# Seven block products in place of eight for the second layer's input projection

## The chip, the cores and the metric

The kernel runs on one core of one Trainium2 chip. The metric is the device time of one execution in microseconds: the median of several runs, lower is better. A profile of one more execution gives the span (from the first to the last instruction) and the trace of every instruction, wait and transfer.

## The reference

A trunk of two residual layers over 512 tokens of 1024 channels, in float32. Each layer computes `x <- x + RMSNorm_post(mixer(RMSNorm_pre(x)))`. The first layer's mixer has two groups of heads (a gated matrix memory and a stick-breaking attention); the change leaves its arithmetic alone. The second layer is what matters here:

```python
def odd_layer(x, pre_g, post_g, w_in, pool_w, pool_scale, w_out):
    h = rmsnorm(x, pre_g)                       # 512 x 1024
    u = h @ w_in                                # 1024 x 4096
    p, z = u[..., :2048], u[..., 2048:]
    pooled = multiscale_pool(p as 4 groups of 512 channels)   # windows 2, 4, 8, 16
    mixed = einsum('bsgc,gce->bsge', pooled, pool_w) * pool_scale
    y = (mixed * silu(z)) @ w_out               # 2048 x 1024
    return x + rmsnorm(y, post_g)
```

`multiscale_pool` subtracts each value from the mean of the last 2, 4, 8 or 16 tokens of its channel.

## The kernel before

Every matrix product is made of three: each float32 operand is kept as two parts in the type float32r, a high part (the value rounded) and a low part (what is left), and `mm3` accumulates high x high, high x low and low x high in PSUM. `split` makes the parts: ACT copies the value into the high tile, which rounds it, and DVE subtracts that from the value into the low tile. For weights, `load` has SP's queue bring a block of 1 MB into one of two `w32` buffers, and `halves` splits a piece of it into one of four pairs of tiles, tagged `wh` and `wl`. A buffer comes free when its last reader is done, and whoever needs it next waits for that.

The code is written for a framework that allocates the tiles, puts in the waits, and orders the instructions of each engine ahead of time with a planner's own model of their costs; each engine then runs its list strictly in that order. `act` adds order among functions that need a table, so that ACT loads each table once for a run of them.

The first layer ends with its output projection (`out_steps`, `out_tile`, L537), in two halves of 256 tokens. `finish_even` then does, for each of four tiles of 128 tokens, the post-norm with the residual (`post`, into `xn`) and the second layer's pre-norm (`prenorm`): square, root, scaling, transposes by TensorE into a PSUM bank with the tag `sc`, and a split into `hTh` and `hTl`, which hold the normed input with channels on the partitions, as eight blocks of 128 channels by 512 tokens.

The second layer runs over four groups, one for each window. A group has four column tiles (128 channels each) of p and four of z. `col_load` loads two column tiles and makes their halves; `col_proj` (L189 to L191, matmuls at L95 to L97) does 8 x 3 matmuls of 128x512 for one tile into one of two `pj` banks. For p, ACT copies the bank into a `win` tile with 16 zeros ahead (L674), and DVE makes the window sums by doubling shifts (L684), mends the first tokens (L689, L690), and subtracts (L691); the result is split into `pph` and `ppl` (tags `phi` and `plo`, six buffers each). For z, `project2` yields the banks and ACT applies Silu into `sz` tiles (six buffers). Then the group's mixing matrix is loaded and split into two pairs, and four products of 4 x 3 matmuls each (`mx`, in `ac` banks) follow, which DVE scales and gates into `y32` (L713). In the first group, whose input is only half there when it begins, p goes over the tokens in two halves of 256 columns. Last come the output projection of the second layer, `finish_odd`, and the stores.

GpSimd (POOL) does masks, memsets and, in the first layer, the running sum of the weights of the matrix memory (L381); its queue issues no transfers. `y32` holds the first layer's output and, later, the second's, as 16 tiles of channels by 512 tokens.

Of the kernel before, what the change touches and what calls it, by code (L numbers as in the profile page):

```python
# [5 lines left out]
F32 = mybir.dt.float32  # L6
# [30 lines left out]
def body(nc, tc, x, pre_g, post_g, w_in, conv, b_i, b_f, hn_g, w_out, w_in_c, pool_w,  # L37
# [6 lines left out]
    with base as base, psum as psum, dram as dram:  # L44
# [10 lines left out]
        # functions that need a table run in the order they are written, so that each  # L55
        # table is loaded once for a run of them
# [21 lines left out]
        def load(parts, a, n, name):  # L78
            """Weights as they come, rows of n columns for each of a row tiles."""
# [25 lines left out]
        # the first layer's input and gate rows stand where its output goes later  # L105
# [8 lines left out]
        # constants  # L114
# [21 lines left out]
        # per-channel vectors, one transpose  # L136
# [24 lines left out]
        def prenorm(xt, xs, tt, gain, name, parts=1):  # L161
# [10 lines left out]
            for half in range(2):  # L172
# [26 lines left out]
        with tc.tile_pool(name="att", bufs=1) as at:  # L199
# [11 lines left out]
            # first pre-norm, and the values of four heads as its tokens come  # L211
# [206 lines left out]
            class Stick:  # L418
                """One head of stick-breaking attention, key blocks from the last to the first."""
# [120 lines left out]
            def y_split(half, c, tiles, name):  # L540
                """Two channel tiles of y, for one half of the tokens."""
# [82 lines left out]
        with tc.tile_pool(name="odd", bufs=1) as od:  # L624
            def gains(g, name):
                t = od.tile([P, D], F32, tag="gain", bufs=2, name=name)
# [3 lines left out]
            def xs(name): return od.tile([P, D], F32, tag="xs", bufs=2, name=name)  # L630

            def ytiles(n):
                return (od.tile([P, S], F32R, tag="phi", bufs=6, name=f"yh_{n}"),
                        od.tile([P, S], F32R, tag="plo", bufs=6, name=f"yl_{n}"))
# [5 lines left out]
            def finish_even(ps, tt):  # L640
                xt = od.tile([P, D], F32, tag="xt", bufs=2, name=f"xe{tt}")
                nc.sync.dma_start(xt, xr[:, tt])
                t = xs(f"xse{tt}")
                post(ps, t, gpo, xt, xn[:, tt], f"e{tt}")
                prenorm(xn[:, tt], t, tt, gpr, f"p1{tt}")
# [7 lines left out]
            gpo1 = gains(post_g[1], "g_post1")  # L653
            for g, w in enumerate(WINDOWS):
                pooled = []
                cur4 = []
                for j in range(4):
# [4 lines left out]
                wj = [w for i in range(2)  # L662
                      for w in col_load(w_in_c[0, :, 512 * g + 256 * i:512 * g + 256 * i + 256], f"p{g}{i}")]
                if g == 0:
                    wj = [w() for w in wj]
                    steps = [(j, wj[j], n) for n in range(2) for j in range(4)]
                else:
                    steps = [(j, wj[j], None) for j in range(4)]
                for j, wt, n in steps:
                    wt = wt() if n is None else wt  # L670
                    n0, n1 = (0, S) if n is None else (256 * n, 256 * n + 256)
# [84 lines left out]
```

## Time and profile before

| | |
|---|---|
| median of 3 runs | 919.13 us (918.66 to 919.36) |
| span of the profiled execution | 916.9 us; with the 2.2 us by which the median stands above it, 919.1 us |
| TensorE busy | 904.5 us (99%), 4453 matmuls |
| DVE, ACT, POOL busy | 533.8, 461.5, 51.9 us |
| mean granted TensorE clock | 0.994 |
| moved by DMA | 98.88 MB, 108 GB/s on average |

The profile's own record of the time is the span; what lies around it (start and end of the program) is only in the runs. A line of the groups reads: source line, engine, operation, output <- inputs, shape, count, then busy time in us and mean duration in ns, then how long the engine had been idle just before these instructions and what ended that. In a timeline the columns are start and length in us. In a row for a stretch of time stand its length, then busy time and count for TensorE, its weight loads, DVE, ACT and POOL, then the granted clock, the busy share of the 16 DMA engines, and GB/s. A row on DMA issues ends with the size and the median time from issue to landing.

### The profile page before, as it was taken

The numbers are of one execution on the slowest core, as the hardware profiler recorded it, in microseconds if no ns is written. First come the engines' busy times: TensorE is split into PE (matmuls) and PEld (weight loads), VectorE is DVE, ScalarE is ACT, GpSimd is POOL, SyncE is SP. The second block draws the span as 40 slices with busy tenths as digits, with TensorE's granted clock in tenths as the row PEclk, the third lists the DMA queues.
The fourth block names the chain that finished last, engine by engine and source line by source line (L and its number), as shares of the span: only waits on it lengthen the run. The fifth ranks groups of instructions, "written<-read, shape, count | busy, mean of one in ns | idle before, by whom it ended". The sixth has DMA issues, their size and how long they took to land.

```text
span 916.9 us, 11439 instructions
## 1 busy us (share of the span) xinstructions
PE 904.5 (99%) x4453; PEld 759.6 (83%) x4453; DVE 533.8 (58%) x817; ACT 461.5 (50%) x766; POOL 51.9 (6%) x189
## 2 busy tenths in 40 slices
PE   8999999999999999999999999999999999999996
PEld 6788889889988898898898878898888888888885
DVE  5435556567876675764764828665462745737542
ACT  6426666766668464464565536553231422335331
POOL 2001111101101101001000000000000000000000
PEclk8999999999999999999999999999999999999999
DMA  8231321212122332324221456624223333326331
GB/s 299 84 101 49 91 85 54 88 51 82 59 92 90 129 93 95 98 78 133 92 87 52 158 183 229 204 78 136 92 91 93 92 92 92 98 87 229 114 115 47
DMA packets 67126, 98.88 MB, mean 108 GB/s; under 512 B 2848, under 2 KB 54136, under 8 KB 67072
## 3 DMA queue, kind: packets, MB, share of 16 engines
q1 hardware_dynamic: 65888, 98.08, 32.9%
q8 instruction: 35, 0.57, 0.3%
q10 hardware_dynamic: 1184, 0.08, 0.1%
q14 instruction: 19, 0.16, 0.1%
HBM read 96.02 MB, written 2.13 MB: 107 GB/s over the span
## 4 chain that ended last, share of the span: by engine, by line
PE 97%; DMA 1%; DVE 1%; ACT 0%; issue 0%; DVEq 0%; POOL 0%; POOLq 0%
PE op L537 10%; PE oq L537 10%; PE ps_z L97 3%; PE ps_qa L97 3%; PE ps_qa L95 3%; PE ps_qa L96 3%; PE ps_z L95 3%; PE ps_z L96 3%; PE ps_p_None L96 2%; PE ps_p_None L95 2%; PE ps_p_None L97 2%; PE psv_va L95 2%; PE psv_va L97 2%; PE psv_va L96 2%; PE ps_zb L95 2%; PE mx L97 2%
## 5 line engine op out<-in xcount | busy, mean ns | idle before, releaser
L97 PE MATMUL ps_qa<-hTh,wl_qa 128*128 128x512 f32 x128 | 50.3, 393 | 0.0
L95 PE MATMUL ps_qa<-hTh,wh_qa 128*128 128x512 f32 x128 | 50.2, 393 | 0.0
L97 PE MATMUL ps_z<-hTh,wl_z 128*128 128x512 f32 x128 | 50.2, 393 | 0.0
L96 PE MATMUL ps_qa<-hTl,wh_qa 128*128 128x512 f32 x128 | 50.2, 392 | 0.0
L95 PE MATMUL ps_z<-hTh,wh_z 128*128 128x512 f32 x128 | 50.2, 392 | 0.0
L96 PE MATMUL ps_z<-hTl,wh_z 128*128 128x512 f32 x128 | 50.2, 392 | 0.0
L71 ACT ACTIVATE wh_p<-w_p 128x1024 fp32r<-128x1024 f32 x16 | 17.0, 1059 | 60.9 <-PE mx L96 31.9
L72 DVE TENSOR_TENSOR wl_wo_e<-w_wo_e,wh_wo_e 128x1024 fp32r<-128x1024 f32 x28 | 34.2, 1232 | 21.9 <-ACT wh_wo_e L71 21.9
L71 ACT ACTIVATE wh_wo_e<-w_wo_e 128x1024 fp32r<-128x1024 f32 x28 | 29.3, 1058 | 30.3 <-DMA w_wo_e<-in_w_out_ab 15.6
L72 DVE TENSOR_TENSOR wl_p<-w_p,wh_p 128x1024 fp32r<-128x1024 f32 x16 | 19.6, 1223 | 35.1 <-ACT wh_p L71 35.1
L537 PE MATMUL op<-wl_wo_e,yh_e 128*128 128x512 f32 x120 | 39.0, 396 | 0.0
L537 PE MATMUL op<-wh_wo_e,yl_e 128*128 128x512 f32 x120 | 38.8, 395 | 0.0
L537 PE MATMUL op<-wh_wo_e,yh_e 128*128 128x512 f32 x120 | 37.8, 396 | 0.0
L95 PE MATMUL ps_p_None<-hTh,wh_p 128*128 128x512 f32 x96 | 37.7, 393 | 0.0
L96 PE MATMUL ps_p_None<-hTl,wh_p 128*128 128x512 f32 x96 | 37.7, 393 | 0.0
L97 PE MATMUL ps_p_None<-hTh,wl_p 128*128 128x512 f32 x96 | 37.7, 392 | 0.0
L67 ACT ACT_TABLE_LOAD x28 | 35.9, 1283 | 1.3 <-PEq L742 0.8
L97 PE MATMUL psv_va<-wh_va,hTl 128*128 128x256 f32 x128 | 36.1, 282 | 0.0
L95 PE MATMUL psv_va<-wh_va,hTh 128*128 128x256 f32 x128 | 36.1, 282 | 0.0
L96 PE MATMUL psv_va<-wl_va,hTh 128*128 128x256 f32 x128 | 36.1, 282 | 0.0
L317 DVE SCALAR_TENSOR_TENSOR cv<-u,vecs,cv 128x511 f32<-128x511 f32 (+2 forms) x48 | 35.4, 748 | 0.4
L72 DVE TENSOR_TENSOR wl_wo_o<-w_wo_o,wh_wo_o 128x1024 fp32r<-128x1024 f32 x20 | 24.2, 1223 | 18.9 <-ACT wh_wo_o L71 18.9
(310 smaller groups left out, 2659.7 us busy)
## 6 DMA issues: line engine op xcount, KB each, us to landing
w_wo_e<-in_w_out_ab SPq DMA_DIRECT2D x14, 1024.0 KB, 4.9
w_wo_o<-in_w_out_c SPq DMA_DIRECT2D x12, 1024.0 KB, 4.7
w_qa<-in_w_in_ab SPq DMA_DIRECT2D x8, 1024.0 KB, 5.0
w_p<-in_w_in_c SPq DMA_DIRECT2D x8, 1024.0 KB, 5.4
w_z<-in_w_in_c SPq DMA_DIRECT2D x8, 1024.0 KB, 5.4
w_qb<-in_w_in_ab SPq DMA_DIRECT2D x4, 1024.0 KB
w_kb<-in_w_in_ab SPq DMA_DIRECT2D x4, 1024.0 KB, 5.0
w_zb<-in_w_in_ab SPq DMA_DIRECT2D x4, 1024.0 KB, 4.9
```

Source lines behind the costliest of these rows:

```text
L67: link(A.preload_act_table_set(TABLE[func]))
L71: A.activation(hi, src, AF.Copy)
L72: V.tensor_tensor(lo, src, hi.bitcast(F32), op=ALU.subtract)
L95: T.matmul(dst, lhsT=ah, rhs=bh, start=first, stop=False, **kw)
L96: T.matmul(dst, lhsT=ah, rhs=bl, start=False, stop=False, **kw)
L97: T.matmul(dst, lhsT=al, rhs=bh, start=False, stop=last, **kw)
L317: V.scalar_tensor_tensor(acc[:, j:], u[:, :S - j], cw(3 - j, c), acc[:, j:], op0=ALU.mult, op1=ALU.add)
L537: T.matmul(ps[a][n], lhsT=l[:, ta], rhs=r[:, 0, n * 512:n * 512 + 512], start=(first and l is yh and r is wh), stop=(last and l is yl))
```

## The change

Strassen's scheme in Winograd's form multiplies two 2 x 2 block matrices with seven block products. Here the blocks are: of a weight block of 1024 x 256, two halves of the rows by its two column tiles (a11, a12, a21, a22, 512 x 128 each); of the input, two halves of the channels by two halves of the tokens (512 x 256 each). The new function `strassen2` computes two column tiles for all tokens with seven `product`s of 4 x 3 matmuls of 128x256, in place of two `col_proj` of 8 x 3 matmuls of 128x512. It is called for z in all four groups and for p in groups 1 to 3, 14 calls. The p of the first group keeps its former form.

- The four sums of weight blocks are formed by POOL into `ws` tiles (three buffers). `first` (a11, a21) and `fourth` (a22) are split as before, by ACT and DVE. `second` and `third`, which are the sums, are split by `halves_dma`: ACT writes the negated rounded sum into the low tile and the rounded sum into the high tile, and a transfer that POOL issues adds the sum to the low tile.
- The four sums of input blocks are formed once, by `hidden_sums`, after the first group's p: DVE adds, `split` makes the parts, in eight `big` tiles. They are formed from unrounded values, which `prenorm` now keeps in unused parts of `y32` with one more ACT copy per half tile (`keep`).
- The products accumulate in turn in two halves of banks, `pa` (`pj`) and `pe` (`xb`), with `pb` (`xa`) for the second. What is in `pa` or `pe` between products is copied out by ACT (`t1`, `t2`, `t5`) or read by DVE while the next product runs into another bank.
- Tiles: `gain`, `xs` and `xt` become one tag `big` with eight buffers; `phi` and `plo` go from six to five, `sz` from six to four; POOL's scratch for transfers is set to 2048. The load of `gpo1` stands behind the last group. The two edge operations of the pooling go from DVE to POOL.

```diff
-        def prenorm(xt, xs, tt, gain, name, parts=1):
+        def prenorm(xt, xs, tt, gain, name, parts=1, keep=None):
...
-                split(tp.rearrange("p (a n) -> p a n", a=4), hTh[dst], hTl[dst])
+                tp = tp.rearrange("p (a n) -> p a n", a=4)
+                split(tp, hTh[dst], hTl[dst])
+                if keep is not None:
+                    A.activation(keep[:, half * 4:half * 4 + 4], tp, AF.Copy)
...
+            def big(name, dtype=F32): return od.tile([P, D], dtype, tag="big", bufs=8, name=name)
...
-                prenorm(xn[:, tt], t, tt, gpr, f"p1{tt}")
+                n0 = tt % 2 * P
+                prenorm(xn[:, tt], t, tt, gpr, f"p1{tt}", 1,
+                        y32[:, tt // 2 * 8:tt // 2 * 8 + 8, n0:n0 + P])
...
+            hs = {"11": hblock(0, 0), "21": hblock(1, 0), "22": hblock(1, 1)}
+
+            def ws(name): return od.tile([P, 8, P], F32, tag="ws", bufs=3, name=name)
+
+            def hidden_sums():
+                raw = {}
+                b11, b21, b12, b22 = quarter(0, 0), quarter(1, 0), quarter(0, 1), quarter(1, 1)
+                for n in ("d3", "d1", "n2", "t4"):
+                    raw[n] = ws(f"raw_{n}")...
+                    hs[n] = [big(f"{n}{e}", F32R).rearrange("p (a n) -> p a n", a=4) for e in "hl"]
+                    if n == "d3":
+                        V.tensor_tensor(raw[n], b22, b12, op=ALU.subtract)
+                    elif n == "d1":
+                        V.tensor_tensor(raw[n], b11, b12, op=ALU.subtract)
+                    elif n == "n2":
+                        V.scalar_tensor_tensor(raw[n], raw["d3"], -1.0, b11, op0=ALU.mult, op1=ALU.subtract)
+                    else:
+                        V.scalar_tensor_tensor(raw[n], raw["n2"], -1.0, b21, op0=ALU.mult, op1=ALU.subtract)
+                    split(raw[n], *hs[n])
+
+            def halves_dma(w, name):
+                n = w.shape[1] * w.shape[2]
+                wh, wl = (t[:, :n] for t in whl(name))
+                w = w.rearrange("p a n -> p (a n)")
+                A.activation(wl, w, AF.Copy, scale=-1.0)
+                A.activation(wh, w, AF.Copy)
+                G.dma_start(wl, w, accum_op=ALU.add)
+                return tuple(t.rearrange("p (a n) -> p a n", n=P) for t in (wh, wl))
+
+            def strassen2(src, name, dsts, silu=False):
+                w = load(lambda t: [(nc.sync, t, src)], 8, 256, name)
+                a11, a12, a21, a22 = (w[:, 4 * k:4 * k + 4, m * P:m * P + P]
+                                      for m in range(2) for k in range(2))
+                sums = [ws(f"ws{i}_{name}") for i in range(2)]
+                s1, s2, s3, s4 = sums[0][:, 4:], sums[0][:, :4], sums[1][:, :4], sums[1][:, 4:]
+                G.tensor_tensor(s1, a21, a22, op=ALU.add)
+                G.tensor_tensor(s2, s1, a11, op=ALU.add)
+                G.tensor_tensor(s3, a11, a21, op=ALU.add)
+                G.tensor_tensor(s4, a12, s2, op=ALU.add)
+                first = halves(w[:, :, :P], f"{name}_a")
+                second, third = (halves_dma(t, f"{name}_{n}") for t, n in zip(sums, "bc"))
+                fourth = halves(a22, f"{name}_d")
+
+                def product(ps, wt, k0, b, start, stop):
+                    (wh, wl), (bh, bl) = wt, hs[b]
+                    for k in range(4):
+                        mm3(ps, (wh[:, k0 + k], wl[:, k0 + k]), (bh[:, k], bl[:, k]),
+                            start and k == 0, stop and k == 3, skip_group_check=True)
+
+                def part(i): return od.tile([P, 256], F32, tag="part", bufs=3, name=f"pt{i}_{name}")
+
+                pa, pb, pe = (f(f"ps{n}_{name}")[:, :256] for f, n in ((pj, "a"), (xa, "b"), (xb, "e")))
+                t1, t2, t5 = part(1), part(2), part(5)
+                product(pa, first, 0, "11", True, True)
+                A.activation(t1, pa, AF.Copy)
+                product(pb, first, 4, "21", True, True)
+                V.tensor_tensor(dsts[0][:, :256], pb, t1, op=ALU.add)
+                product(pa, second, 0, "n2", False, True)
+                A.activation(t2, pa, AF.Copy)
+                product(pe, second, 4, "d1", True, True)
+                A.activation(t5, pe, AF.Copy)
+                product(pa, third, 0, "d3", False, True)
+                V.scalar_tensor_tensor(dsts[1][:, 256:], pa, -1.0, t5, op0=ALU.mult, op1=ALU.subtract)
+                product(pe, third, 4, "22", False, True)
+                V.tensor_tensor(dsts[0][:, 256:], pe, t2, op=ALU.add)
+                product(pa, fourth, 0, "t4", False, True)
+                if silu:
+                    act(dsts[0], dsts[0], AF.Silu)
+                    act(dsts[1][:, 256:], dsts[1][:, 256:], AF.Silu)
+                    act(dsts[1][:, :256], pa, AF.Silu, scale=-1.0)
+                else:
+                    A.activation(dsts[1][:, :256], pa, AF.Copy, scale=-1.0)
...
-                    steps = [(j, wj[j], None) for j in range(4)]
-                for j, wt, n in steps:
-                    wt = wt() if n is None else wt
...
+                    hidden_sums()
                 else:
+                    for i in range(2):
+                        strassen2(wsrc[i], f"p{g}{i}", [t[:, 16:] for t in cur4[2 * i:2 * i + 2]])
...
-                    V.tensor_tensor(sm[:, :e], sm[:, :e], invc[:, :e], op=ALU.mult)
-                    V.tensor_tensor(sm[:, :e], sm[:, :e], p32[:, :e], op=ALU.subtract)
+                    G.tensor_tensor(sm[:, :e], sm[:, :e], invc[:, :e], op=ALU.mult)
+                    G.tensor_tensor(sm[:, :e], sm[:, :e], p32[:, :e], op=ALU.subtract)
...
-                for j, ps in enumerate(p for i in range(2) for p in project2(
-                        w_in_c[0, :, 2048 + 512 * g + 256 * i:2304 + 512 * g + 256 * i], f"z{g}{i}")):
...
+                for i in range(2):
+                    pair = [od.tile([P, S], F32, tag="sz", bufs=4, name=f"sz{4 * g + 2 * i + j}")
+                            for j in range(2)]
+                    strassen2(w_in_c[0, :, 2048 + 512 * g + 256 * i:2304 + 512 * g + 256 * i],
+                              f"z{g}{i}", pair, True)
+                    sz.extend(pair)
...
+            gpo1 = gains(post_g[1], "g_post1")
...
-                t, q = xs(f"xo{tt}"), od.tile([P, D], F32, tag="xt", bufs=2, name=f"xq{tt}")
+                t, q = big(f"xo{tt}"), big(f"xq{tt}")
...
+                    dynamic_dma_scratch_size=2048)
```

More of the change, by code (lines that the diff above doesn't have):

```diff
@@ L625, in gains @@
             def gains(g, name):
[L626 removed]
+                t = big(name)
                 nc.sync.dma_start(t, g.partition_broadcast(P))
                 return t
[L630 removed]
+            def big(name, dtype=F32): return od.tile([P, D], dtype, tag="big", bufs=8, name=name)
             def ytiles(n):
[L633 to L634 removed]
+                return (od.tile([P, S], F32R, tag="phi", bufs=5, name=f"yh_{n}"),
+                        od.tile([P, S], F32R, tag="plo", bufs=5, name=f"yl_{n}"))
             ready = y_split(1, EVEN2[0], ytiles("first"), "e")
@@ L651, in body, with quarter, hblock @@
                       lambda a: finish_even(ps1[a], 2 + a))
-            gpo1 = gains(post_g[1], "g_post1")
+            def quarter(k, n): return y32[:, 8 * n + 4 * k:8 * n + 4 * k + 4, 0:256]
+            def hblock(k, n):
+                ix = (slice(None), slice(4 * k, 4 * k + 4), slice(256 * n, 256 * n + 256))
+                return hTh[ix], hTl[ix]
+            hs = {"11": hblock(0, 0), "21": hblock(1, 0), "22": hblock(1, 1)}
+            def ws(name): return od.tile([P, 8, P], F32, tag="ws", bufs=3, name=name)
```

29 lines of the change are left out of this document (12 added, 17 removed).

## The prediction

> **What bounds the kernel now.** I read the page's totals first, then the chain, then TensorE's own waits.
>
> ```profile
> span 916.9 us, 11439 instructions
> PE 904.5 (99%) x4453; PEld 759.6 (83%) x4453; DVE 533.8 (58%) x817; ACT 461.5 (50%) x766; POOL 51.9 (6%) x189
> PEclk8999999999999999999999999999999999999999
> PE 97%; DMA 1%; DVE 1%; ACT 0%; issue 0%; DVEq 0%; POOL 0%; POOLq 0%
> ```
>
> TensorE is busy for 99% of the span, its clock is granted in full, and the chain that ended last is TensorE for 97%. The second layer's projections lie between 594.8 and 814.5 us. Two whole groups of that stage, and TensorE's waits (total, times, longest):
>
> ```profile
> 666.84:777.72 110.88, 110.88 (x481) 90.21 (x481) 55.65 (x82) 33.21 (x44) 2.45 (x22) 1.00 0.32 95
> PE tp_p L179 <- DVE y L174: 1.6, 1, 1.6
> PE ps_p L95 <- ACT hTh L71: 0.2, 1, 0.2
> PE ps_p L96 <- DVE hTl L72: 0.2, 1, 0.2
> ```
>
> In that stretch TensorE (second column) never pauses, while DVE is busy 50%, ACT 30%, POOL 2%, and the DMA engines 0.32. So time taken from TensorE here is time taken from the kernel, as long as the others keep up. A matmul's duration (393 ns in the page) is no price, since matmuls overlap; the distance between starts is. From the chain in order of time, the same matmul of three successive groups:
>
> ```profile
> 666.84 0.24 PE ps_p_None L96
> 722.28 0.24 PE ps_p_None L96
> 777.72 0.24 PE ps_p_None L96
> ```
>
> A group has 96 + 96 + 48 = 240 matmuls of 512 columns and takes 55.44 us: 0.231 us each. For 256 columns, the first group's input projection, in two stretches of the timeline:
>
> ```profile
> 594.79 0.28 PE L95 MATMUL ps_p<-hTh,wh_p 128*128 128x256 f32 x1
> 601.35 0.28 PE L96 MATMUL ps_p<-hTl,wh_p 128*128 128x256 f32 x1
> 609.36 0.28 PE L97 MATMUL ps_p<-hTh,wl_p 128*128 128x256 f32 x1
> 620.60 0.28 PE L97 MATMUL ps_p<-hTh,wl_p 128*128 128x256 f32 x1
> ```
>
> 55 steps in 6.56 us and 93 in 11.24: 0.119 and 0.121. I take 0.120. Weights are loaded for each matmul there too, so the smaller shape costs 4% more per column and no more.
>
> **The change, part by part.** *Matmuls.* A pair of column tiles took 48 x 0.231 = 11.09 us. It becomes seven products of 12 matmuls, 1.44 us each: 84 x 0.120 = 10.08 us. `strassen2` is called 6 times for p (groups 1 to 3) and 8 times for z. Saved at most: 14 x 1.01 = 14.1 us. The first group's p stays as it is.
>
> *Work on the other engines.* Prices:
>
> ```profile
> L72 DVE TENSOR_TENSOR wl_z<-w_z,wh_z 128x1024 fp32r<-128x1024 f32 x16 | 19.6, 1224 | 14.2 <-ACT wh_z L71 14.1
> L71 ACT ACTIVATE wh_z<-w_z 128x1024 fp32r<-128x1024 f32 x16 | 17.0, 1061 | 35.8 <-PE ps_p_None L96 21.2 <-PE ps_p L96 7.5 <-issue 7.1
> L72 DVE TENSOR_TENSOR ppl<-p,pph 128x512 fp32r<-128x512 f32 x16 | 11.0, 687 | 3.5 <-ACT pph L71 3.5
> L71 ACT ACTIVATE pph<-p 128x512 fp32r<-128x512 f32 x16 | 10.0, 625 | 15.6 <-DVE p L690 15.6
> L68 ACT ACTIVATE sz<-ps_z 128x512 f32<-128x512 f32 x16 | 9.3, 579 | 0.0
> L674 ACT ACTIVATE p<-ps_p 128x256 f32<-128x256 f32 x8 | 3.0, 373 | 2.7 <-PE ps_p L97 2.7
> L72 DVE TENSOR_TENSOR vl_va<-psv_va,vh_va x16: 405/420/425, 239.0 to 475.9; 128x256 fp32r<-128x256 f32 x16
> ```
>
> ACT in a p call: five copies of 128x1024 (`first`, and two each for `second` and `third`) 5.3, one of 128x512 0.63, three partial copies and the last one 1.5: 7.4 us. A z call adds the Silu of a whole tile and a half, 0.95: 8.4 us of 10.08. Before it was 3.3 per pair. DVE: 1.22 + 0.69 and three 128x256 operations out of PSUM at 0.42, 3.2 against 2.45. POOL, with adds so far only in the first layer:
>
> ```profile
> 413.37 1.01 POOL L381 TENSOR_TENSOR w<-w,w 128x384 f32<-128x384 f32 x1 [45.28 <-DVE pl L72]
> 418.04 0.74 POOL L381 TENSOR_TENSOR w<-w,w 128x256 f32<-128x256 f32 x1 [3.66 <-DVE w L367]
> 420.27 0.46 POOL L381 TENSOR_TENSOR w<-w,w 128x128 f32<-128x128 f32 x1 [1.21 <-DVE w L367]
> 298.86 1.22 DVE L72 TENSOR_TENSOR wl_qa<-w_qa,wh_qa 128x1024 fp32r<-128x1024 f32 x1
> 299.09 1.58 POOL L381 TENSOR_TENSOR w<-w,w 128x256 f32<-128x256 f32 x1 [1.05 <-DVE w L367]
> 299.99 0.96 DVE L72 TENSOR_TENSOR pl<-w,ph 128x256 fp32r<-128x256 f32 x1
> ```
>
> 0.275 us per 128 columns gives 1.29 for 128x512: four adds 5.2 us per call, plus two DMA issues. No engine is over its 10.08, so on averages the 14.1 would be all gained. What decides is order.
>
> *The ring of four weight pairs.* A call takes four `wh`/`wl` pairs and there are four. `second` serves products 3 and 4: its pair comes free after four products and is needed by the next call after nine, so five products, 7.2 us, lie between; the same for `first` and `third`, six for `fourth`. `first` and `fourth` need ACT and DVE, 2.3 us, and are covered. `second` and `third` need a chain L: the partial copy that ACT does first (0.4), the negated copy (1.06), POOL free to issue, the accumulating DMA from issue to landing. A period is then the larger of 10.08 and L + 2.88; at L = 8.2 it is the old 11.09. No accumulating DMA, nor any from POOL's queue, is in the trace. The nearest:
>
> ```profile
> w_z<-in_w_in_c SPq DMA_DIRECT2D x8, 1024.0 KB, 5.4
> xe<-in_x SPq DMA_DIRECT2D x4, 512.0 KB, 6.1
> out<-xo SPq DMA_DIRECT2D x8, 256.0 KB, 3.0
> L83 SPq DMA_DIRECT2D w_z<-in_w_in_c x8: 367/368/368, 591.7 to 770.1; - x8
> ```
>
> Its 512 KB are read twice and written once. Lower end 3.0 (the store of 256 KB), upper end 6.1 (a load of 512 KB amid others). I take 5.4, the row whose 1024 KB equal what this one reads. With half an add, 0.65, of waiting at POOL, L = 0.4 + 1.06 + 0.65 + 5.4 = 7.5, the period 10.38, the loss 14 x 0.30 = 4.2 us; by the ends L is 5.1 (no loss) to 8.2 (14.1, all of the gain). The Trainium skill's "DMA: Bandwidth & Descriptors" (section "Anatomy of one DMA — SWDGE (gpsimd) path") fits a transfer issued by POOL as 2.0 us plus its bytes at 436 GB/s, an estimate of 3.2 us for 512 KB. By that nothing would be late and the sum would end 4.2 us lower; no run here shows such a DMA yet.
>
> *PSUM handed on inside a call.* `pa` and `pe` are read out while the next product runs in another bank, 1.44 us for each of five turns. The read is 0.37 to 0.42; behind one 1.06 to 1.22 operation already running it takes up to 1.64, so 0 to 0.2 late a turn. This runs within the slack that the 10.38 already has, so I add nothing; without it, it would cost up to 14 x 0.3.
>
> *The start.* The last token tile's pre-norm is just too late already:
>
> ```profile
> 606.14 0.60 ACT L71 ACTIVATE hTh<-tp_p 128x512 fp32r<-128x512 f32 x1
> 607.76 1.09 ACT L71 ACTIVATE hTh<-tp_p 128x512 fp32r<-128x512 f32 x2
> 608.39 1.29 DVE L72 TENSOR_TENSOR hTl<-tp_p,hTh 128x512 fp32r<-128x512 f32 x2 [0.93 <-ACT hTh L71]
> 608.41 0.50 PE L95 MATMUL ps_p<-hTh,wh_p 128*128 128x256 f32 x2 [0.24 <-ACT hTh L71]
> ```
>
> The new `keep` copies put 0.6 us on ACT behind each `hTh`, and hold the `sc` bank as long. A copy between the two last `hTh` delays only blocks 4 to 7, 1.4 us of matmuls later; one before them delays all: 0 to 1.2, I take 0.6. `hidden_sums` needs 8 DVE operations of 1.22 (9.8 us) and 4 ACT copies from 609.7 on, of which the third product needs six, 7.3 us, by 620.7 + 2.9 = 623.6. That fits. But the raw sums hold the three `ws` buffers, so the first call's weight sums start some 5 us in: 609.7 + 5 + two adds 2.6 + 1.06 + 5.4 is 623.8, and `third` is later by the wait for t4. 0 to 4, I take 1.5.
>
> *What costs nothing, and its cover.* SP's weight load waits for a `w32` that `fourth` releases some 1.4 us into the call before the last; it lands at 6.8, and the adds have until 15.8, 9 us for 5.2 (uncovered: 5.4 a call). Behind a POOL issue that waits for ACT's copy stand the next adds and memsets; they share those 9 us. The edges (two small operations per tile) go from DVE to POOL; the pooled halves are not needed until the mixing product, a 20 us z stage later. `gpo1`'s load must wait until the `big` buffers of the hidden sums are free, after the last z; 11 us of mixing and 44 us of output projection lie before its first use (else 6.1). Five `phi`/`plo` and four `sz` still hold one group. The DMA engines' share rises from 0.32 by 0.3 to 0.7 at most.
>
> *Sum.* Span 916.9 - 14.1 + 4.2 + 0.6 + 1.5 = 909.1. The median of the runs, 919.13, is 2.2 above the span of the profiled execution; I keep these 2.2: **911.3, say 911 us**.
>
> **The rivals.** *All is hidden.* L stays under 7.2: 919.1 - 14.1, and 0 to 2.1 for the start: 905 to 907. For it the low DMA end and 5.2 us of POOL work; against it ACT at 8.4 of 10.08, whose copies must come just as a pair falls free.
>
> *POOL and DVE hold each other up.* The add at 299.09 beside two DVE subtractions took 1.58 instead of 0.74, and the second subtraction 0.96 instead of 0.42. So an add of 1.29 becomes 2.1, and a read-out by DVE behind a stretched subtraction 0.42 + 1.22 + 0.54 = 2.2 in a turn of 1.44: 0.74 late. One such turn a call makes the period 10.82 and the time 919.1 - 14.1 + 10.4 + 2.1 = 917.5; the case runs from 914 to 921. Against it: both engines together are busy for little more than half of a period. The Trainium skill's "SBUF — State Buffer" (section "Who interferes with whom") says that a DVE instruction with two SBUF inputs blocks a GpSimd instruction that reads SBUF wholly until it ends. By that rule with every add blocked by a whole 1.22, POOL would need 4 x 2.51 + 0.74 = 10.8 a call, the same time; the 0.84 lost above agrees in kind.
>
> *The accumulating DMA is late and it ends slower.* Place: products 3 and 5 of each call. It decides from L = 8.06 on (with 2.1 lost at the start, 0.86 a call is all there is). With a whole add ahead at POOL and the 6.1 row: 0.4 + 1.06 + 1.29 + 6.1 = 8.85, a period of 11.73, 919.1 + 9.0 + 2.1 = 930 us. For it: no such DMA is in the trace, and its source is beside weight loads; against it the 256 KB row.
>
> *The change doesn't do what it says:* 256-column matmuls would have to cost 0.132 us; both stretches above say 0.12.
>
> **How the numbers follow.** Forecast (907 to 914) 0.38; all hidden 0.22; POOL against DVE 0.20; DMA late 0.16; no effect 0.04. A measurement of this kernel tells about 0.2%, 1.8 us, from no change. Faster than 917.3 are the first two and 0.12 of the third, 0.72; within it 0.08 of the third and the last, 0.12; slower 0.16. The range goes from 904.5 (0.1195 us per matmul, nothing lost) to 920 and leaves out the late DMA.
>
> **What would show it.** Right: the 256-column matmuls of `strassen2` 0.12 us apart, calls 10.1 to 10.6 us long, TensorE's waits few and put down to the accumulating DMA before products 3 and 5, ACT near 80% in the z calls, POOL near 60%. Wrong: waits on ACT or DVE at every turn (handing on), adds of 2 us (POOL against DVE), landings over 6 us (late DMA), a gap of several us near 621 (start), or another order of calls than the one assumed, which a planner chooses from its own costs.

## The result, and the profile after

The changed kernel takes 961.65 us (median of 4 runs, 961.1 to 964.03) against 919.25 for the kernel before beside it: a ratio of 1.0463 (95% interval 1.0448 to 1.0478). It is slower by 42 us; 911 was forecast.

The totals, the granted clock in 40 slices and the chain, from the profile of the changed kernel:

```profile
span 959.4 us, 12835 instructions
PE 908.3 (95%) x4957; PEld 785.7 (82%) x4957; DVE 583.3 (61%) x835; ACT 528.9 (55%) x878; POOL 176.5 (18%) x305
PEclk8999999999999999999999999989989999889999
PE 78%; DMA 10%; DVE 5%; POOL 4%; issue 2%; ACT 1%; SPq 0%; DVEq 0%; POOLq 0%; ACTq 0%
```

TensorE fell from 97% of the chain to 78%; DMA, DVE and POOL took its place. Next the stage from the first group's last p product to the output projection, before and after (length; busy time and count of TensorE, its weight loads, DVE, ACT and POOL; granted clock; DMA share; GB/s):

```profile
620.70:814.70 194.00, 194.00 (x843) 157.91 (x842) 99.47 (x148) 61.74 (x82) 4.01 (x36) 1.00 0.32 98
```
```profile
621.60:857.40 235.80, 197.92 (x1345) 184.34 (x1345) 142.64 (x167) 121.50 (x184) 123.77 (x150) 0.93 0.59 145
```

All of the loss is here: 235.8 - 194.0 = 41.8 us. What precedes it became 0.9 longer, what follows 0.2 shorter (959.4 - 857.4 = 102.0 against 102.2). With the 14.1 us saved, the stage would be 179.9. Of the 55.9 us above that, 37.9 are pauses of TensorE (235.80 - 197.92). In the other 18 it is busy for longer with the same work, mostly because the clock is lower: it is granted at half for 30.7 us of the stage, TensorE is busy for 25.6 of these, and half of that, 12.8, is lost. For the rest there is only an estimate: a matmul is recorded as 0.28 us long and starts 0.12 after the one before, so each of the 25 pauses adds about 0.16 of busy time, 4 us in all. TensorE's waits in this stage (total, times, longest):

```profile
PE psa_z L97 <- DMA wl_z_b<-ws_z: 20.7, 6, 6.5
PE psa_z L97 <- DMA wl_z_c<-ws_z: 5.8, 4, 3.1
PE psa_z L97 <- DVE wl_z_a L72: 4.2, 4, 1.8
PE psa_p L97 <- DMA wl_p_c<-ws_p: 2.8, 5, 0.7
PE psa_p L97 <- DMA wl_p_b<-ws_p: 1.4, 3, 0.6
```

Products 3 and 5 wait for the accumulating DMA, as in the rival that ends slower, but nearly only in the z calls. Is the transfer slow? Issues in the stage, with the median from issue to landing:

```profile
wl_z_b<-ws_z POOLq DMA_DIRECT2D x8, 512.0 KB, 4.6
wl_z_c<-ws_z POOLq DMA_DIRECT2D x8, 512.0 KB, 6.1
wl_p_b<-ws_p POOLq DMA_DIRECT2D x6, 512.0 KB, 5.2
wl_p_c<-ws_p POOLq DMA_DIRECT2D x6, 512.0 KB, 5.5
```

No: on the median it is what was assumed (5.4). It is issued late. ACT and POOL in the first z call of the second group (start, length):

```profile
682.59 1.06 ACT L694 ACTIVATE wh_z_b<-ws_z 128x1024 fp32r<-128x1024 f32 x1 [1.01 <-PE pse_p L96]
683.82 1.05 ACT L693 ACTIVATE wl_z_b<-ws_z 128x1024 fp32r<-128x1024 f32 x1
```
```profile
687.78 0.19 POOL L776 TENSOR_TENSOR p<-p,invc 128x3 f32<-128x3 f32 x1 [1.43 <-DVE p L771]
...
689.29 1.28 POOL L705 TENSOR_TENSOR ws_z<-w_z 128x512 f32<-128x512 f32 x1 [1.27 <-DMA w_z<-in_w_in_c]
690.53 0.20 POOL L777 TENSOR_TENSOR p<-p,p 128x3 f32<-128x3 f32 x1
690.67 0.89 POOL L695 DMA_DIRECT2D wl_z_b<-ws_z  x1
691.27 1.60 POOL L706 TENSOR_TENSOR ws_z<-ws_z,w_z 128x512 f32<-128x512 f32 x1
692.50 0.42 POOL L770 MEMSET p<- 128x16 f32 x1
695.25 1.27 POOL L707 TENSOR_TENSOR ws_z<-w_z 128x512 f32<-128x512 f32 x1 [2.33 <-DMA wl_z_b<-ws_z]
696.48 1.73 POOL L708 TENSOR_TENSOR ws_z<-w_z,ws_z 128x512 f32<-128x512 f32 x1
698.16 0.87 POOL L695 DMA_DIRECT2D wl_z_c<-ws_z  x1
```

The negated copy ends at 684.87; the transfer is issued at 690.67, 5.8 us later. Ahead of it in POOL's list stand edge operations that wait for DVE, and the next call's first weight sum, which waits for its load. The transfer of `third` then stands behind two more sums of the next call, the first of which needs the `ws` buffer that the transfer of `second` reads, and that comes free when this has landed (695.2). In the four groups the issue of `second` follows its copy by 5.1, 5.8, 6.0 and 6.1 us in the first z call; in the first group it is this call's own third and fourth sum, 1.7 and 2.2 us long, that stand ahead. In the second z call it follows by 0.4 to 1.5; there, in the three later groups, the landing is long instead (8.1, 8.9 and 6.6 us). From 700 to 714 us:

```profile
w_p<-in_w_in_c SPq DMA_DIRECT2D x1, 1024.0 KB, 7.7
wl_z_b<-ws_z POOLq DMA_DIRECT2D x1, 512.0 KB, 8.1
wl_z_c<-ws_z POOLq DMA_DIRECT2D x1, 512.0 KB, 7.4
```

Both transfers of the call are under way at once there, beside loads by SP. Besides, when the first is issued (702.50), its queue is still moving the transfer of `third` of the call before, which was itself issued late (698.16) and sends its last packet until 703.8. And the clock, which had been granted in full: behind such a wait,

```profile
694.20:698.30 4.10, 3.26 (x16) 3.07 (x15) 4.07 (x5) 1.21 (x2) 3.05 (x3) 0.50 0.11 20
```

it is 0.50, here until 700.9, 6.8 us in all, and the 256-column matmuls start some 0.21 us apart in place of 0.12. The stage has six such stretches, three of 3.4 us and three of 6.8; in the 3.4 us before each of them TensorE had been busy for 1.7 at most. The Trainium skill's "TensorE: Matmul & The Clock Gate" (section "Part 1: The HAM clock gate") says that the clock halves after an idle window of about 3.4 us and comes back after a busy one. The trace agrees in the lengths, but only in one of the six cases had TensorE been idle for the whole 3.4 us before, and a pause of 3.6 us (to 777.82) has no such stretch behind it.

### The profile page after: what moved, and what is told of

Same layout as the page of the kernel before. It is cut to its first block, busy times and chain, and to the rows that moved or that the text cites. A ratio compares the mean times of both kernels' runs of the same rounds, so it can differ in the third digit from the quotient of the medians.

```text
span 959.4 us, 12835 instructions
## 1 busy us (share of the span) xinstructions
PE 908.3 (95%) x4957; PEld 785.7 (82%) x4957; DVE 583.3 (61%) x835; ACT 528.9 (55%) x878; POOL 176.5 (18%) x305
## 3 DMA queue, kind: packets, MB, share of 16 engines
HBM read 96.02 MB, written 2.13 MB: 102 GB/s over the span
## 4 chain that ended last, share of the span: by engine, by line
PE 78%; DMA 10%; DVE 5%; POOL 4%; issue 2%; ACT 1%; SPq 0%; DVEq 0%; POOLq 0%; ACTq 0%
PE op L540 9%; PE oq L540 9%; DMA wl_z_b<-ws_z 3%; PE ps_qa L97 3%; PE ps_qa L95 3%; PE ps_qa L96 3%; DMA wl_p_c<-ws_p 2%; DMA w_z<-in_w_in_c 2%; PE psv_va L97 2%; PE psv_va L95 2%; PE psv_va L96 2%; PE ps_zb L95 2%; PE ps_oa L96 2%; PE ps_oa L97 2%; PE ps_za L95 2%
## 5 line engine op out<-in xcount | busy, mean ns | idle before, releaser
L384 POOL TENSOR_TENSOR w<-w,w 128x384 f32<-128x384 f32 (+2 forms) x12 | 10.4, 870 | 144.1 <-DVE pl L72 135.3
L447 POOL TENSOR_SCALAR_AFFINE_SELECT a<-a 128x128 f32<-128x128 f32 x32 | 12.1, 387 | 126.9 <-DVE a L445 111.3
L771 DVE TENSOR_TENSOR p<-p 128x512 f32<-128x512 f32 x40 | 30.8, 775 | 3.5 <-POOL p L770 2.5
L97 PE MATMUL psa_z<-n2h,wl_z_b 128*128 128x256 f32 x32 | 12.7, 396 | 20.7 <-DMA wl_z_b<-ws_z 20.7
L71 ACT ACTIVATE wh_wo_o<-w_wo_o 128x1024 fp32r<-128x1024 f32 x20 | 20.9, 1052 | 19.3 <-PE oq L540 9.1
L72 DVE TENSOR_TENSOR wl_qa<-w_qa,wh_qa 128x1024 fp32r<-128x1024 f32 x16 | 19.6, 1223 | 18.4 <-ACT wh_qa L71 18.4
L540 PE MATMUL oq<-wl_wo_o,yh_o 128*128 128x512 f32 x96 | 30.5, 395 | 0.0
L540 PE MATMUL oq<-wh_wo_o,yl_o 128*128 128x512 f32 x96 | 30.3, 395 | 0.0
```

What stands on the lines that cost most here:

```text
L71: A.activation(hi, src, AF.Copy)
L72: V.tensor_tensor(lo, src, hi.bitcast(F32), op=ALU.subtract)
L97: T.matmul(dst, lhsT=al, rhs=bh, start=False, stop=last, **kw)
L384: G.tensor_tensor(total[:, t0:], total[:, t0:], w[:, t0:], op=ALU.add)
L447: G.affine_select(a[:, t0:t0 + P], a[:, t0:t0 + P], pattern=[[1, P]], base=-1, channel_multiplier=-1, compare_op=ALU.is_ge, fill=0.0)
L540: T.matmul(ps[a][n], lhsT=l[:, ta], rhs=r[:, 0, n * 512:n * 512 + 512], start=(first and l is yh and r is wh), stop=(last and l is yl))
```

## The experiments

Three causes were on the table. Q: the issue of the transfer is stuck in POOL's list. D: the transfer itself is late. L: POOL's and DVE's two-input operations hold each other up. Each time stands beside the kernel before on the same chip (918.8 to 919.4), so a difference between two experiments can hold some 0.6 us that come from the chips. An edit also lets the planner order all lists anew, and the time holds that too.

**e1: the edges of the pooling back on DVE.**

```diff
-                    G.tensor_tensor(sm[:, :e], sm[:, :e], invc[:, :e], op=ALU.mult)
-                    G.tensor_tensor(sm[:, :e], sm[:, :e], p32[:, :e], op=ALU.subtract)
+                    V.tensor_tensor(sm[:, :e], sm[:, :e], invc[:, :e], op=ALU.mult)
+                    V.tensor_tensor(sm[:, :e], sm[:, :e], p32[:, :e], op=ALU.subtract)
```

> The pooling's two edge operations go back to DVE; all else as in the changed kernel. Theory Q (POOL's queue: the accumulating DMA is issued late because edge operations and weight sums stand ahead of it): the lag between ACT's negated copy and the issue, 5.1 to 6.1 us in the first z call of each group, falls to 2 us or less where the edges made it, the waits on wl_z_b fall from 22 to some 14 us, the time to 945 to 953. Theory D (the DMA itself takes too long for the ring): lag or not, the time stays within 3 us of 961. If the lag stays because the sums that wait for the weight load make it, the time stays too, and the next kernel decides.

Measured: 964.59 us (ratio 1.0493, 1.0472 to 1.0514). The issue still comes 5.7 to 5.9 us late in the later groups. The edges are not the cause; with them on POOL it is even 3 us faster.

**e2: weight sums and edges on DVE; the transfers stay.**

```diff
-                G.tensor_tensor(s1, a21, a22, op=ALU.add)
...
+                V.tensor_tensor(s1, a21, a22, op=ALU.add)
...
```

(all four sums, and the edges as in e1)

> Weight sums and edge operations on DVE: POOL keeps only the issues of the 28 accumulating DMAs and memsets. Theory Q: every lag is under 0.6 us, only the second z calls of a group are still late, TensorE's waits in the stage fall from 43 to under 20 us, the time to 930 to 940. Theory D: landings of 8 to 10 us in the second z calls stay and the first calls become late for the same reason; waits stay over 30 us and the time over 948. Theory L (POOL's sums and DVE lock each other out): DVE operations are back at their old lengths (0.69 for 128x512), but this alone moves TensorE little.

Measured: 926.06 us (1.0074, 1.0054 to 1.0094). The issues follow their copies by 0.35 us (two by about 1.0). TensorE's waits for transfers:

```profile
PE psa_z L97 <- DMA wl_z_b<-ws_z: 3.3, 1, 3.3
PE pse_z L97 <- DMA wl_z_b<-ws_z: 3.0, 2, 1.7
PE psa_z L97 <- DMA wl_z_c<-ws_z: 2.6, 2, 1.3
PE psa_p L97 <- DMA wl_p_c<-ws_p: 2.6, 2, 1.7
```

With the sums gone from POOL, 38.5 us of e1 come back, 4 us more than Q expected. That fits Q and L alike.

**e3: no accumulating DMA (`second` and `third` are split as `first` is); sums and edges stay on POOL.**

```diff
-                second, third = (halves_dma(t, f"{name}_{n}") for t, n in zip(sums, "bc"))
+                second, third = (halves(t, f"{name}_{n}") for t, n in zip(sums, "bc"))
```

> No accumulating DMA: the parts of the summed weights are made by ACT and DVE as those of plain weights are (ACT rounds, DVE subtracts); sums and edges stay on POOL. If the DMA chain (its queue at POOL or its landing) is the cause, TensorE's waits fall from 43 us to under 8 and the time to 906 to 914, faster than the kernel before. If POOL's sums beside DVE are the cause (theory L), DVE subtractions of 2 to 4 us keep the weights late and the time stays over 925.

Measured: 933.81 us (1.0161, 1.0146 to 1.0176). Without any transfer 27.8 us of the changed kernel's time are back, but it is still 14.8 over the kernel before: the transfers can't be all, and POOL's sums alone turn the gain into a loss.

**e4: both, so that DVE does sums, low parts and edges.**

> No accumulating DMA, and sums and edges on DVE: POOL has memsets alone. Per call DVE then has three subtractions of 1.22, one of 0.69, three read-outs of 0.42 and four sums of 0.69, 8.4 us of 10.08 without the pooling. If seven products in themselves are as cheap as predicted, 905 to 912. If the turns in PSUM or ACT's load are a cause beside the DMA, waits on ACT and DVE take the place of those on the DMA and the time stays over 919.

Measured: 916.2 us (median of 7 runs; 0.9969, 0.9957 to 0.998), faster than before, but 4 us above the range that was expected if seven products are as cheap as predicted. The scheme pays once nothing of it is on POOL; sums and transfers each have to go.

**e5: e1, with the next call's sums behind this call's issues in POOL's list.** An order alone; no work is moved.

```diff
+            issued = []
...
-                G.dma_start(wl, w, accum_op=ALU.add)
+                issued.append(G.dma_start(wl, w, accum_op=ALU.add))
...
-                G.tensor_tensor(s1, a21, a22, op=ALU.add)
+                one = G.tensor_tensor(s1, a21, a22, op=ALU.add)
...
-                G.tensor_tensor(s3, a11, a21, op=ALU.add)
+                three = G.tensor_tensor(s3, a11, a21, op=ALU.add)
+                for i in issued[-2:]:
+                    for s in (one, three):
+                        tc.add_manual_dep(s.ins, i.ins.name, NOSYNC, reason="sums behind the issues")
```

> The kernel with the edges on DVE (964.6 us), with one more thing fixed: the next call's weight sums stand behind this call's two DMA issues in POOL's queue. POOL does the same work, DVE and POOL meet as often, the DMAs are the same. Theory Q (the issue stands behind sums that wait for their load): in the first z call of each group the issue follows the end of ACT's negated copy by under 1.5 us in place of 5.7 to 5.9, the waits of 46 us lose about 5 us in each of the three groups and the half-clock stretches behind them go too: 935 to 950 us. Theory L (POOL and DVE slow each other): no change, 960 to 968 us, with the DVE subtractions as long as before. Theory D (the transfers themselves): no change either, because the landings of the second z calls, 8 to 10 us, stay.

Measured: 952.01 us (950.18 to 957.38; 1.0374, 1.0345 to 1.0402): 12.6 us of e1's time are back, 2 us short of what Q expected and far from no change. In the first z calls of the four groups the issue of `second` now follows its copy by 4.0, 0.4, 2.5 and 3.7 us (4.0, 5.7, 5.9 and 5.9 in e1): the lag is smaller, not gone, since this call's own fourth sum and memsets that wait for DVE still stand ahead. The landings in the second z calls of the later groups, which were to stay by D, fell too, from 4.9 to 10.8 us down to 4.5 to 5.1. TensorE's largest waits:

```profile
PE psa_z L97 <- DMA wl_z_b<-ws_z: 9.0, 3, 6.4
PE psa_p L97 <- DVE wl_p_a L72: 6.8, 3, 2.7
PE psa_z L97 <- DVE wl_z_a L72: 4.7, 5, 2.2
```

The wait for the transfer of `second` fell from 21.0 (e1) to 9.0, most of it in the first call. What remains is now on DVE, in the low part of `first`, which has neither a DMA nor a sum before it. In one p call of each later group that subtraction takes 4.3 to 4.7 us in place of 1.22, while POOL runs its four additions:

```profile
669.26 4.73 DVE L72 TENSOR_TENSOR wl_p_a<-w_p,wh_p_a 128x1024 fp32r<-128x1024 f32 x1 [0.21 <-ACT wh_p_a L71]
```

That is L. So Q is real, and not all.

**e6: e3 with the edges on DVE,** the missing corner of four.

> Sums on POOL, edges on DVE, no accumulating DMA: the missing corner of four (sums on POOL or DVE, low parts by DMA or DVE, edges on DVE in all): 964.6, 926.1, this one, 916.2. If POOL's sums and the DMAs each cost what they cost alone, this would be 964.6 - (926.1 - 916.2) = 954.7 us. Theory Q (they hurt through the one queue): close to the same kernel with the edges on POOL, 930 to 935 us, so that POOL's sums alone cost 14 to 19 us (theory L's part: sums that are late and DVE operations that are stretched) and the DMA behind them in the queue some 30 us more against 10 us without them.

Measured: 937.94 us (1.0201, 1.0185 to 1.0217), 3 us above what Q expected and 17 below plain addition. With the edges on DVE in all four:

| | low parts by DVE | low parts by DMA |
|---|---|---|
| sums on DVE | 916.2 (e4) | 926.1 (e2) |
| sums on POOL | 937.9 (e6) | 964.6 (e1), 952.0 in e5's order |

Sums on POOL cost 21.7 us by themselves, the transfers 9.9, and both together 48.4, which is 16.8 more than the two. The order of e5 alone gives 12.6 us back: most of the extra hangs on what stands in which order in POOL's list. By which path it does is not separated: the lag, the landings and DVE all changed in e5. One more thing shows only where both are on POOL: in e1 three DVE subtractions are 4.0 us longer than alone (4.7 in place of 0.69), while in e6, with the same additions and no transfers, no DVE addition or subtraction is more than 1.1 longer.

**e7: e2 with ACT's negated copy first.** In the changed kernel the planner had put the high copy (L694) ahead, as at 682.59 above.

```diff
-                A.activation(wl, w, AF.Copy, scale=-1.0)
-                A.activation(wh, w, AF.Copy)
+                low = A.activation(wl, w, AF.Copy, scale=-1.0)
+                high = A.activation(wh, w, AF.Copy)
+                tc.add_manual_dep(high.ins, low.ins.name, NOSYNC, reason="low part first")
```

> The kernel with sums and edges on DVE and the accumulating DMAs kept (926.1 us), with ACT's negated copy ahead of the high copy. The negated copy ends 1.06 us sooner in each piece, so every issue too. Theory D with the landing as the late one (second z calls 8.5 to 10.1 us from issue to use): about 1 us less of wait at each of the three second z calls and at some of the others, 921 to 925 us. If the ends are set by the load that collides and not by the issue: no change, 925.5 to 926.5 us. The high part is late by 1.06 us in its place, which could show as waits for it.

Measured: 922.48 us (median of 9; 1.0037, 1.0025 to 1.0049), 3.6 us better than e2, as expected.

**e8: e4 with the first z call of group 0 written ahead of that group's pooling.**

> The kernel with sums, low parts and edges on DVE (916.2 us), with the first z call of group 0 written ahead of the pooling of that group, so that DVE does its halves first. It lost 2.1 + 2.5 us there at 625 and 627 us and about 2.6 us at half clock behind them. If DVE's order sets these waits: 909 to 913 us. If the pooling that is moved back makes the group's mixing wait for its inputs: 915 to 918 us, with waits for the pooled tiles at about 650 us.

Measured: 916.06 us (0.9965, 0.9952 to 0.9979): no change. The planner still puts pooling operations among the call's sums, and TensorE's two waits there stay (1.8 and 1.9 us, in e4 1.8 and 2.3).

**e9: e4 with four idle additions on POOL in each call.** Their result goes to a tile that is overwritten later.

```diff
+                for i in range(4):
+                    G.tensor_tensor(y32[:, 15].rearrange("p (a n) -> p a n", a=4), a21, a22, op=ALU.add)
                 first = halves(w[:, :, :P], f"{name}_a")
```

> The kernel with sums, low parts and edges on DVE (916.2 us), plus four additions on POOL in each call, of the same shape and from the same loaded weights, whose result nobody uses: POOL then works as it does with the sums on it, but no sum is late and no issue stands in its queue. Sums on POOL cost 937.9 - 916.2 = 21.7 us without the DMA. Theory L (POOL's additions slow DVE while they run): most of the 21.7 comes back, 928 to 940 us, with DVE's groups stretched as there (pooling additions 873 ns on the mean in place of 686). Its rival, that the sums on POOL are simply late (four of 1.3 to 2 us in place of four of 0.69, 3 to 5 us before each second and third piece): 915 to 920 us, with DVE's means near those of the kernel without them.

Measured: 964.9 us (1.0498, 1.0484 to 1.0512), 48.7 more than e4, beyond even what L expected, for results that nobody uses. DVE and then POOL at the start:

```profile
616.67 2.31 DVE L72 TENSOR_TENSOR d3l<-raw_d,d3h 128x1024 fp32r<-128x1024 f32 x1
618.91 2.31 DVE L72 TENSOR_TENSOR d1l<-raw_d,d1h 128x1024 fp32r<-128x1024 f32 x1
621.14 2.32 DVE L72 TENSOR_TENSOR wl_z_a<-w_z,wh_z_a 128x1024 fp32r<-128x1024 f32 x1
```
```profile
615.75 14.94 POOL L710 TENSOR_TENSOR y<-w_z 128x512 f32<-128x512 f32 x7
```

The same three DVE operations in e4:

```profile
615.30 1.22 DVE L72 TENSOR_TENSOR d3l<-raw_d,d3h 128x1024 fp32r<-128x1024 f32 x1
616.43 1.22 DVE L72 TENSOR_TENSOR d1l<-raw_d,d1h 128x1024 fp32r<-128x1024 f32 x1
617.57 1.22 DVE L72 TENSOR_TENSOR wl_z_a<-w_z,wh_z_a 128x1024 fp32r<-128x1024 f32 x1
```

The two engines take turns here: each DVE operation is longer by nearly one addition (1.22 becomes 2.31), and each addition by most of a DVE operation (14.94 / 7 = 2.13 in place of 1.27 alone). The Trainium skill's "SBUF — State Buffer" (section "Who interferes with whom") states that rule, an exclusive lock for two-input DVE operations against GpSimd's reads; in this stretch the trace agrees, operation by operation. Over the stage of e4 and of e9:

```profile
622.40:811.20 188.80, 181.48 (x1341) 172.74 (x1340) 171.03 (x279) 98.00 (x156) 4.01 (x36) 0.98 0.33 104
```
```profile
622.70:861.00 238.30, 198.08 (x1340) 185.35 (x1339) 224.83 (x284) 98.39 (x157) 92.96 (x88) 0.91 0.26 83
```

DVE's busy time grew by 53.8 us, 0.96 for each of 56 additions, and the stage by 49.5. DVE is busy 91% of e4's stage and 94% of e9's, so it has no slack; in the changed kernel it is busy 60%. e9 shows the lock and its price for a DVE without slack, not that the changed kernel loses 48.7 by it; there, e6 gives 21.7, and that holds sums that are merely late as well.

**e10: e8 with the first pooling addition of group 0 ordered behind the low part of `second`.**

In the diff, `lows` lists the low-part subtractions in the order in which they are written; the third from the end is that of `second`.

```diff
+                    if j == 0:
+                        behind = lows[-3] if g == 0 else None
...
+                        if behind is not None:
+                            tc.add_manual_dep(step.ins, behind.ins.name, NOSYNC, reason="first z call ahead")
```

> The kernel with everything on DVE and the first z call written ahead of the pooling (916.06 us): moving the text changed nothing, since the planner still put the group's pooling into DVE's queue among the call's sums (pooling additions at 619.0, 621.3, 622.0, 625.0 us; the low part that TensorE waits for ends at 629.1 us). Here the first pooling addition of that group stands behind that low part by an order given by hand. Five DVE instructions of 0.15 to 0.69 us (2.9 us in all) come off the path: the waits of 2.1 and 2.3 us at 624 and 627 us shrink by some 2.5 to 4 us, and the half-clock stretch behind (2.3 us) with them: 910 to 914 us. If the pooling is then late for the group's mixing: 915 to 919 us.

Measured: 912.67 us (911.42 to 913.3, 5 runs; 0.9926, 0.9913 to 0.994), the fastest version, 6.7 us faster than before. Its stage:

```profile
621.20:806.10 184.90, 179.33 (x1341) 170.57 (x1339) 170.58 (x280) 97.55 (x156) 4.01 (x36) 1.00 0.33 106
```

The clock is whole again, and the stage 9.1 us shorter than before (in the profiled execution, which is 1.3 us below the median). The largest wait left is 2.4 us, for the last pooled tile of the last group.

**e11: e7 with the transfers in the p calls alone;** in the z calls DVE makes the low parts.

```diff
+                second, third = ((halves if silu else halves_dma)(t, f"{name}_{n}") for t, n in zip(sums, "bc"))
```

> Sums and edges on DVE, ACT's negated copy first, and the accumulating DMA kept for the p calls alone (12 of 28); in the z calls DVE makes the low parts. Between all DMAs (922.5 us) and none (916.2 us). Theory D, narrowed: the DMA costs where it meets the load of the pool weights (the second z call of each group) and in the first call, and nothing in the p calls, whose weights are used 5 to 8 us after the issue with hardly a wait: 914 to 918 us, no wait for a DMA of wl_p over 1 us. If each DMA costs its share: 922.5 - 16/28 x 6.3 = 918.9 us or more.

Measured: 922.15 us (919.02 to 925.09; 1.0029, 1.0013 to 1.0045), no better than e7. A miss: there is no wait for a transfer, yet the 6 us over e4 remain. Of these, 3.7 are small waits elsewhere (11.2 us of waits in the stage, 7.5 in e4), most of them here:

```profile
PE psa_z L97 <- DVE wl_z_a L72: 2.8, 4, 1.5
PE psa_z L95 <- ACT pt_z L729: 0.9, 2, 0.5
PE pse_z L95 <- ACT pt_z L731: 0.8, 1, 0.8
```

It may be that DVE and ACT come later to the turn from p to z under another plan; no run shows it. What a transfer costs in each place is not settled by this.

**e12: e9 with one idle addition per call.**

> As the run with four idle additions on POOL in each call (964.9 us, 48.7 us over the 916.2 us without), but with one in each call, 14 in all in place of 56. If an addition on POOL costs by the time that it runs beside DVE, each is worth 48.7 / 56 = 0.87 us: 928 us (924 to 933). If only a pile of them hurts, because DVE catches up between calls after a single one: 915 to 919 us. The TensorE waits should be in the first piece's and the second piece's weights in either case.

Measured: 925.35 us (1.007, 1.0053 to 1.0087): 9.2 us for 14 additions, 0.65 each, a quarter less than the 0.87 of e9 (48.7 / 56). A single addition is not absorbed.

## Why the prediction was wrong, step by step

**The saved matmuls: right.** The matmuls of undisturbed products of the changed kernel start 0.119 us apart, 16 steps in 1.91 us:

```profile
689.79 0.28 PE L95 MATMUL psa_p<-t4h,wh_p_d 128*128 128x256 f32 x1
691.70 0.28 PE L95 MATMUL psa_z<-n2h,wh_z_b 128*128 128x256 f32 x1
```

e10 shows 6.7 of the 14.1 us.

**POOL's list: the step that failed.** Under "What costs nothing" the prediction asked what stands behind an issue that waits, and let the adds share 9 us of slack. It did not ask what stands ahead of the issue: the next call's sums, which wait for a load and for a `ws` buffer that a transfer still reads. The term "POOL free to issue" in L, set at 0.65, was 5.1 to 6.1 in the first z calls (up to 7.7 for `third`). The same chain then gives L = 0.4 + 1.06 + 1.06 + 5.8 + 4.6 = 12.9 there, well over the break-even at 8.06. e5 changes this order alone and gets 12.6 us back, and by the table of four what the two cost together beyond their own prices is 16.8. It is not the largest term of the loss: that is POOL against DVE, below, which the sum put at nothing.

**The landing: right on the median, wrong in the second z calls** (8.1, 8.9 and 6.6 where 3.0 to 6.1 had been the bounds), where transfers of POOL's queue overlap with each other and with SP's loads. In e5, with the issues in another order, these landings are 4.5 to 5.1, so the late issue has a share in them. **The copies' order:** L counted the negated copy alone; the planner put the high copy first in nearly all pieces, 1.06 more; e7 prices that at 3.6 us in all for e2's kernel. The estimate of 3.2 us from the Trainium skill's "DMA: Bandwidth & Descriptors" (section "Anatomy of one DMA — SWDGE (gpsimd) path") is below every row here; the shortest landing in the changed kernel is 4.4.

**POOL against DVE: the mechanism was right as a rival, the size and the place were not.** The sum put it at nothing, since the handing on in PSUM was to run within the slack; the rival priced it at one late read-out a call, 10.4 us. The sums on POOL cost 21.7 (e6 against e4). The place is not the hand-over in PSUM but the subtraction for a low part. In the changed kernel one of 128x512 took

```profile
679.10 4.73 DVE L72 TENSOR_TENSOR wl_p_d<-w_p,wh_p_d 128x512 fp32r<-128x512 f32 x1
```

in place of 0.69, and one such in each of the three later groups. It does not wait for one turn but for three additions in a row:

```profile
679.19 1.60 POOL L706 TENSOR_TENSOR ws_z<-ws_z,w_z 128x512 f32<-128x512 f32 x1
680.44 1.59 POOL L707 TENSOR_TENSOR ws_z<-w_z 128x512 f32<-128x512 f32 x1
681.68 1.59 POOL L708 TENSOR_TENSOR ws_z<-w_z,ws_z 128x512 f32<-128x512 f32 x1
```

Why DVE gets no turn between them, as it does in e9, no run shows. "Both engines together are busy for little more than half of a period" was no argument against it: POOL's sums come in one burst when their load lands, here from 677.33 to 683.3, and what DVE does just then is stretched.

**The late DMA, the rival that came true,** had its place right (products 3 and 5) and was priced at 930, from a whole add of waiting and one landing. It lacked POOL's list, the lock on top of it, and the clock.

**The clock: left out.** The full clock of the profile before was carried over as if it were given. It held in the stage of the kernel before, where TensorE never paused, and in e10, where no pause is longer than 2.4 us; the changed kernel's pauses, up to 6.5 us, brought six stretches at half clock, and some 13 us of the loss are matmuls that run slowly there.

**Right or small:** the edges on POOL (e1), `gpo1` (102.0 us against 102.2 after the stage), and the copies for `keep`, priced at 0.6 (the stage starts 0.9 later).

**The start: too low.** The first z call, priced at 1.5, has 7.2 us of waits in the changed kernel (0.7, and 6.5 for the transfer of `second`, the longest of the stage): POOL's list again. With nothing on POOL it is 3.7 in e8 (1.8 and 1.9) and 1.6 in e10: then it depends on DVE's order there.

**Still open:** how the 16.8 us that sums and transfers cost beyond their own prices divide among the lag, the landings and DVE's long subtractions, and, of the 9.9 us of the transfers alone, the 6 that e7 leaves, since in e11 they stayed when 16 of 28 transfers were gone.

## What to carry to other kernels

A transfer that POOL issues is as late as the slowest wait ahead of it in POOL's list, here by up to 7.7 us: before putting one there, write out what stands ahead of it and what each of those waits for, not only the engine's load. Work moved from DVE to POOL was not work in parallel here, where both read two operands from SBUF: each addition of 1.3 us on POOL cost 0.65 to 0.87 us of the kernel's time beside a DVE with little slack (e12, e9). And a TensorE at full clock must be priced with its clock: here 37.9 us of pauses brought some 13 us of slow matmuls with them, a third as much again.

## What was not expected of the hardware

- A granted clock of 0.50 for 3.4 or 6.8 us behind waits, six times in one stage; the kernel before has none in it.
- Turns between POOL and DVE in e9, where 1.22 becomes 2.31 and 1.27 becomes 2.13, operation by operation; but no turn for a 128x512 subtraction in the changed kernel, which takes 4.73 us behind three additions.
- The first packet of an accumulating transfer of 512 KB comes 1.45 us after its issue when nothing else is under way, and 3.07 us after it (702.50 to 705.57) while an earlier transfer of POOL's queue (until 703.8) and a load of 1 MB by SP are. With a load alone under way it was 1.97 once (issue at 831.72); how much each adds is open.
